# Splitting the mixers' projection weights in the first block only, and loading both parts from device memory afterwards

## The chip, the cores and the metric

The kernel runs on one core of a Trainium2 chip. The metric is the device time of one launch in microseconds (us); the time before is the median of three runs. A core has five engines that each work through an instruction list of their own: PE (TensorE, matrix multiplication), DVE (VectorE), ACT (ScalarE), POOL (GpSimd) and SP (SyncE, which here issues nearly all DMAs). They meet at semaphores. DMAs bring data between device memory and the on-chip memory (SBUF); PE writes its sums into PSUM.

## The reference

One layer of a streaming encoder, for a prompt of 2048 rows and a sample of 32 rows, each row 1024 wide:

```
xn   = rms_norm(x);  proj = xn @ w_in          # 1024 x 2176
u_a, u_b, u_c, u_d = split(proj)               # 512, 896, 256, 512 columns
y_a = conv module(u_a)      # gate, causal depthwise conv of width 31, layer norm, swish
y_b = RWKV-7 mixer(u_b)     # token shift, decay, delta-rule state, 4 heads of 64
y_c = pooling mixer(u_c)    # trailing means of 2/4/8/16 rows
y_d = window attention(u_d)
x   = x + concat(y_a, y_b, y_c, y_d) @ w_out   # 1024 x 1024
x   = x + (silu(rms_norm(x) @ gate) * (rms_norm(x) @ up)) @ down
```

The outputs are both x and the caches and states of both. All values are float32.

## The kernel before

**Three products for one.** A float32 operand is written as a rounded part and a remainder (`hi` and `lo`, type fp32r), and `mm3` (line 92) computes hi·hi + hi·lo + lo·hi. Every weight and every activation that enters such a product has to be split first: ACT copies the raw values to the fp32r type, which rounds them, and another engine subtracts the copy from the raw values.

**Stages.** The mixers come first, then the feed-forward part in two stages (gate and up; down). The mixer stage walks over the prompt in eight blocks of 256 rows (`TB`, line 46); the sample rides along in block 1. In every block the whole of `w_in` and the whole of `w_out` is needed again. They are taken in units: one unit is 1024 rows by 256 columns (128 columns for one of them), read by `load_unit` (line 358) in two halves of 512 rows, that is, of four k-slices of 128 rows. A block has 13 units: four in `proj_b` (line 439; mixer B's columns, the first unit with 128 columns), five in `proj` (line 474: two for attention in `qkv_half`, two for the convolution, one for pooling), four in `out_proj` (line 1056).

**One unit.** `load_unit` loads each half into a tile `wraw` (three buffers). For each pair of k-slices it allocates `whi` and `wlo` (four buffers each, which hold one unit), has ACT copy `wraw` to `whi` (line 370) and POOL subtract (line 373) to get `wlo`. Three of the subtractions of the first two units are given to DVE (`LV0`, line 75). So a half is one DMA, two ACT instructions and two POOL instructions, and a full one is 128 partitions by 4 by 256 values, 512 KB. The tiles are given back when PE has done its last matmul with them. In `transposed` (line 423) PE goes through all eight k-slices for the first 128 columns and then through all eight again for the next 128; in `qkv_half` through all eight for the first 128 rows of the block and again for the next; in `out_proj` (`KO` = 4) both row tiles use the first half before the second half is touched.

**Order.** The letters of `ORD` (line 68) give the order in which a block's parts are written down: `proj` of block b, recurrence of b, norm and `proj_b` of b+1, preparation of the recurrence of b+1, `out_proj` of b−1, then attention preparation, pooling, convolution, output of mixer B, attention of b. Thus two to three blocks are under way at once. A planner that is part of the program's framework then orders every engine's instructions, by priorities and by a timeline of its own. The splits stand under a raised priority (`EVP`). The DMAs of SP are issued in the planner's order, one after the other, and each waits for its target buffer.

**Neighbours on DVE.** The convolution (line 551) is 60 `scalar_tensor_tensor` instructions a block, each reading two tiles in SBUF. The solve of the recurrence's preparation (lines 830, 833, 835) is some 60 small instructions a block, again with two SBUF inputs. Results of the projections are taken from PSUM by ACT and DVE (lines 461 to 466, 509 to 517, 1091).

Of the kernel before, what the change touches and what calls it, by code (L numbers as in the profile page):

```python
# [8 lines left out]
F32 = mybir.dt.float32  # L9
F32R = mybir.dt.float32r  # L10
BF16 = mybir.dt.bfloat16
AF = mybir.ActivationFunctionType
# [5 lines left out]
ADD, SUB, MUL, MAX = ALU.add, ALU.subtract, ALU.mult, ALU.max  # L18
# [14 lines left out]
def layer(tc, ins, outs):  # L33
    nc = tc.nc
    V, S, G, TE = nc.vector, nc.scalar, nc.gpsimd, nc.tensor
# [3 lines left out]
    KT = D // 128  # L39
# [19 lines left out]
    LOV = ()  # L59
    RP = ""  # L60
    YB = 1
    WR = 3
    WH = 4
    YT = "rk"
    KH = 8
    KI = 8
# [9 lines left out]
    HG = 2  # L76
# [15 lines left out]
    def mm3(out, ah, al, bh, bl, first, last, more=False):  # L92

        TE.matmul(out, ah, bh, start=first, stop=False, skip_group_check=more)  # L94
        TE.matmul(out, ah, bl, start=False, stop=False, skip_group_check=more)  # L95
        TE.matmul(out, al, bh, start=False, stop=last, skip_group_check=more)  # L96

    def mm2(out, ahl, bh, bl, first, last):
        TE.matmul(out, ahl, bh, start=first, stop=False)  # L99
        TE.matmul(out, ahl, bl, start=False, stop=last)  # L100

    def add2(acc, ps):

        V.tensor_tensor(acc, acc, ps[0:DS], op=ADD)
        V.tensor_tensor(acc, acc, ps[DS:2 * DS], op=ADD)

    dpool = ctx.enter_context(tc.tile_pool(name="dram", bufs=1, space=DRAM))
# [41 lines left out]
    b3 = p1.enter_context(tc.tile_pool(name="b3", bufs=2, side="left"))  # L149
# [88 lines left out]
    for e in range(2):  # L238
        o = 64 * e
# [35 lines left out]
    for g, w in enumerate(WINS):  # L275
        o = 64 * (g % 2)
# [15 lines left out]
    for sg in (seg_p, seg_s):  # L292
        sg.mask = tri_mask("tri" + sg.name, sg.CPT, sg.L)
        n = sg.NC * (sg.L + 1)
# [35 lines left out]
    for e in range(2):  # L330
        o = 64 * e
# [23 lines left out]

    nun = [0]

    def load_unit(dma, n):
        parts = []
        dv = LV0[nun[0]] if nun[0] < len(LV0) else LOV  # L360
        nun[0] += 1
        for j in range(0, KT, 4):
            raw = b3.tile([128, 4, 256], F32, tag="wraw", name="wraw", bufs=WR)
            dma(raw, j)
            for i in range(0, 4, HG):
                hi = b3.tile([128, HG, 256], F32R, tag="whi", name="whi", bufs=WH)
                lo = b3.tile([128, HG, 256], F32R, tag="wlo", name="wlo", bufs=WH)
                src = raw[:, i:i + HG, :n]
                with tc.high_priority(offset=EVP):
                    S.activation(hi[:, :, :n], src, AF.Copy)  # L370
                    for q in range(0, HG, 2):
                        e = V if (j + i + q) // 2 in dv else G
                        e.tensor_tensor(lo[:, q:q + 2, :n], src[:, q:q + 2], hi[:, q:q + 2, :n].bitcast(F32), op=SUB)  # L373
                parts.append((hi, lo))
        return lambda k, w: (parts[k // HG][0][:, k % HG, w], parts[k // HG][1][:, k % HG, w])

    def load_win(c0, n):
        return load_unit(lambda r, j: nc.sync.dma_start(
            r[:, :, :n], w_in[j * 128:j * 128 + 512, c0:c0 + n].rearrange("(k p) c -> p k c", p=128)), n)

    ysx = c1.tile([128, 8, 2 * DS], F32R, name="ysx")
# [12 lines left out]
    def sgs(b, o):  # L394
        return [sg for sg in (seg_p, seg_s) if at_block(sg, b, o)]
# [27 lines left out]
    def transposed(b, xh, xl, res, c0, nm, evac):  # L423
        W = TB + DS if b == SB else TB
        wt = load_win(c0, nm * 128)
        pss = {}
        for k0 in range(0, KT, KH):
            for m in range(nm):
                if k0 == 0:
                    pss[m] = pmm.tile([128, 512], F32, tag="mm", name="pj")  # L430
                ps = pss[m]
                for k in range(k0, k0 + KH):
                    mm3(ps[:, :W], *wt(k, slice(m * 128, (m + 1) * 128)), xh[:, k, :W], xl[:, k, :W], k == 0, k == KT - 1)
                if k0 + KH == KT:
                    for sg in segs(b):
                        with tc.high_priority(offset=EVP):
                            evac(sg, res[sg.name], m, ps[:, sg.col:sg.col + sg.T])
# [618 lines left out]
    def out_proj(b, ys):  # L1056
        for q in range(D // 256):
            cw = slice(q * 256, q * 256 + 256)

            def dma(raw, j):  # L1060
                if j == 0:
                    nc.sync.dma_start(raw, w_out[0:512, cw].rearrange("(k p) c -> p k c", p=128))
                    return
                nc.sync.dma_start(raw[:, 0:2, :], w_out[512:768, cw].rearrange("(k p) c -> p k c", p=128))
                for kv in range(2):
                    nc.sync.dma_start(raw[64 * kv:64 * kv + 64, 2:4, :],
                                      w_out[768 + 128 * kv:896 + 128 * kv, cw].rearrange("(g d) c -> d g c", d=64))
            wt = load_unit(dma, 256)
            pss = {}
            for k0, sg, i in ((k0, sg, i) for k0 in range(0, KT, KO) for sg in sgs(b, "O") for i in range(sg.NT)):  # L1070
                PT = sg.PT
                if k0 == 0:
                    src = x_s if sg is seg_s else x_p[b * TB + i * 128:b * TB + i * 128 + 128]
                    xr = b3.tile([128, 256], F32, tag="xr", name="xr", bufs=XRB)
                    nc.sync.dma_start(xr[:PT], src[:, cw])
                    pss[sg.name, i] = pmm.tile([128, 512], F32, tag="mm", name="po"), xr
                ps, xr = pss[sg.name, i]
                cs = slice(i * 128, i * 128 + PT)
                for k in range(k0, k0 + KO):
                    if sg is seg_s:  # L1080
                        mm2(ps[:2 * DS, :256], ysx[:, k, :], *wt(k, slice(0, 256)), k == 0, k == 7)
                        continue
                    yh, yl = ys["abcd"[k // 2]]
                    mm3(ps[:PT, :256], yh[:, k % 2, cs], yl[:, k % 2, cs], *wt(k, slice(0, 256)), k == 0, k == 7)
                if k0 + KO == KT:
                    dst = x2d[SEQ:SEQ + DS] if sg is seg_s else x2d[b * TB + i * 128:b * TB + i * 128 + 128]
                    with tc.high_priority(offset=EVP):
                        if sg is seg_s:
                            add2(xr[:PT], ps[:, :256])
                        else:  # L1090
                            V.tensor_tensor(xr[:PT], ps[:PT, :256], xr[:PT], op=ADD)
                    nc.sync.dma_start(dst[:, cw], xr[:PT])
# [8 lines left out]
    for b in range(NB):  # L1101
        ys = y_tiles()
        cur = res
        for o in ORDS[max(b - NB, -len(ORDS))]:
          with tc.high_priority(offset=OFF[o]) if o in OFF else ExitStack():
            if o == "R":
                ro = mix_b(b, cur, ys)
            if o == "Y":
                mix_y(ro, ys)
            if o == "O" and pend is not None:  # L1110
                out_proj(*pend)
            if o == "A":
                proj(b, cur, *xhl)
            if o == "P":
                mix_p(b, cur)
            if o == "D":
                mix_d(b, cur, ys)
            if o == "C":
                mix_a(b, cur, ys)
            if o == "L":  # L1120
                mix_c(b, cur, ys)
            if o == "n" and b + 1 < NB:
                xn = norm_load(b + 1)
            if o == "N" and b + 1 < NB:
                xhl = norm(b + 1, xn)
            if o == "B" and b + 1 < NB:
                res = proj_b(b + 1, *xhl)
            if o == "S" and b + 1 < NB:
                for sg in sgs(b + 1, "R") if SEP else [seg_p]:
                    rwkv_prep(sg, rs(sg, res))  # L1130
        pend = (b, ys)
    out_proj(*pend)
    p1.close()

# [179 lines left out]
    for hf in range(D // 512):  # L1314
        w = slice(hf * 512, hf * 512 + 512)
        with tc.high_priority(offset=FNP):
            dws = [down_w(f, w) for f in range(NF)]
        for t in range(TT // 128 + 1):
            n = min(128, TT - t * 128)
# [4 lines left out]
            lo = ah[:, :, n:2 * n] if n == DS else al[:, :, :n]  # L1324
# [56 lines left out]
```

## Time and profile before

| | |
|---|---|
| median of the runs shown | 2809.56 us (three runs, 2804.55 to 2813.81) |
| the profiled execution's own time | 2805.44 us |
| its span, first to last instruction | 2803.7 us |
| mean granted TensorE clock | 0.946 of full speed |
| HBM read, written | 267.69 MB, 40.96 MB |
| DMA packets | 399678, 311.46 MB, mean 111 GB/s |

Span and own time differ by 1.7 us, which lie around the first and the last instruction. A profile row names the source line, the engine, the operation, the tiles written and read, and shapes; then the busy time in us with the mean of one instruction in ns, or, in the views of one tile or one line, the smallest, median and largest duration in ns with the first and last start in us. `wraw`, `whi`, `wlo` are the tiles of the weights; `pj`, `pjd` and `po` the PSUM tiles of `transposed`, `qkv_half` and `out_proj`; `accp` is the convolution's sum, `dn` and `gu` belong to the feed-forward part. A letter p or s behind a name stands for prompt or sample. Idle time stands behind the engine that sat idle, with what ended it.

### The profile page before, as it was taken

To read this page: it belongs to the slowest core of one execution; us is meant where nothing else is said; L and a number is where in the kernel's file an instruction comes from. 1 tells how busy PE (TensorE), PEld (TensorE's weight loads), DVE (VectorE), ACT (ScalarE), POOL (GpSimd) and SP (SyncE) were. 2 spreads that over 40 slices of the span, in tenths; PEclk is the share of its full clock that TensorE was granted. 3 is DMA by queue.
4 is the path that set the end of the run, shared out by engine and by line. 5 is a ranking of instruction groups with operands and counts; after the bars stand their busy time and mean duration, and the time that the engine had idled before them with its cause. 6 is when DMAs were issued, how large, how long until landed. Compare 5 with 4: busy or idle time off the path is not lost. (4 is left out here: it accounts for less than half of the span.)

```text
span 2803.7 us, 44493 instructions
## 1 busy us (share of the span) xinstructions
PE 2525.5 (90%) x16433; PEld 2276.9 (81%) x16433; DVE 1959.7 (70%) x3629; ACT 1152.6 (41%) x2389; POOL 1427.4 (51%) x1093
## 2 busy tenths in 40 slices
PE   7888797888988898886999989999899969999999
PEld 6777676777877787775899989999899967887887
DVE  7897969898797979975877777777766633224221
ACT  5445354453545445454444444444444432112110
POOL 5545545564555655565677757677677720001000
PEclk9889888899999999997999989999999989999999
DMA  4323322332334332435334323333233366446442
GB/s 149 93 62 98 98 85 86 117 99 86 110 103 120 102 102 92 120 110 158 94 108 131 104 81 107 121 103 100 87 114 106 95 180 187 124 118 180 133 125 54
DMA packets 399678, 311.46 MB, mean 111 GB/s; under 512 B 23282, under 2 KB 372739, under 8 KB 399459
## 3 DMA queue, kind: packets, MB, share of 16 engines
q1 hardware_dynamic: 397848, 307.99, 36.7%
q8 instruction: 129, 2.11, 0.3%
q10 hardware_dynamic: 1611, 0.62, 0.1%
q14 instruction: 90, 0.74, 0.1%
HBM read 267.69 MB, written 40.96 MB: 110 GB/s over the span
## 5 line engine op out<-in xcount | busy, mean ns | idle before, releaser
L1223 POOL TENSOR_TENSOR wl<-wf,wh 128x512 fp32r<-128x512 f32 x462 | 665.1, 1444 | 248.9 <-ACT wh L1222 237.8
L373 POOL TENSOR_TENSOR wlo<-wraw,whi 128x512 fp32r<-128x512 f32 (+1 forms) x413 | 566.7, 1391 | 418.4 <-ACT whi L370 341.7
L94 PE MATMUL gu<-xh,wh 128*128 128x352 f32 (+1 forms) x1848 | 595.1, 323 | 27.8 <-ACT xh L1187 18.3
L96 PE MATMUL gu<-xh,wl 128*128 128x352 f32 (+1 forms) x1848 | 597.8, 324 | 0.0
L95 PE MATMUL gu<-xl,wh 128*128 128x352 f32 (+1 forms) x1848 | 595.3, 322 | 0.7 <-DVE xl L1188 0.7
L1222 ACT ACTIVATE wh<-wf 128x512 fp32r<-128x512 f32 x462 | 290.3, 631 | 466.2 <-PE gu L95 397.8
L94 PEld LDWEIGHTS gu<-xh,wh 128*128 128x128 f32 x1848 | 350.0, 190 | 30.2 <-ACT xh L1187 19.2
L95 PEld LDWEIGHTS gu<-xl,wh 128*128 128x128 f32 x1848 | 350.6, 190 | 1.0 <-DVE xl L1188 0.9
L96 PEld LDWEIGHTS gu<-xh,wl 128*128 128x128 f32 x1848 | 350.1, 189 | 0.2
L370 ACT ACTIVATE whi<-wraw 128x512 fp32r<-128x512 f32 (+1 forms) x416 | 247.7, 611 | 196.4 <-PE po L96 68.7
L551 DVE SCALAR_TENSOR_TENSOR accp<-gbp,d_cws,accp 128x256 f32<-128x256 f32 x480 | 308.3, 674 | 0.6
L94 PE MATMUL dn<-dw,ah 128*128 128x512 f32 x704 | 275.1, 392 | 25.0 <-ACT dw L1310 23.7
L96 PE MATMUL dn<-dw,al 128*128 128x512 f32 x704 | 275.0, 391 | 0.9 <-DVE al L1328 0.9
L95 PE MATMUL dn<-dw,ah 128*128 128x512 f32 x704 | 274.2, 391 | 0.0
L94 PE MATMUL pj<-xh,whi 128*128 128x256 f32 (+1 forms) x832 | 253.5, 308 | 14.2 <-DVE gbp L512 7.0
L96 PE MATMUL pj<-xh,wlo 128*128 128x256 f32 (+1 forms) x832 | 250.8, 310 | 13.5 <-POOL wlo L373 13.3
L95 PE MATMUL pj<-xl,whi 128*128 128x256 f32 (+1 forms) x832 | 249.5, 304 | 0.1
L1340 DVE TENSOR_TENSOR xr<-xr,dn 128x512 f32<-128x512 f32 x32 | 22.0, 687 | 306.2 <-PE dn L96 306.2
L1327 ACT ACTIVATE ah<-af 128x1408 fp32r<-128x1408 f32 (+1 forms) x68 | 86.5, 1321 | 362.1 <-PE dn L95 340.2
L94 PEld LDWEIGHTS pj<-xh,whi 128*128 128x128 f32 x832 | 171.0, 206 | 26.0 <-DVE gbp L512 7.5
L96 PEld LDWEIGHTS pj<-xh,wlo 128*128 128x128 f32 x832 | 167.9, 205 | 26.9 <-POOL wlo L373 18.5
L94 PEld LDWEIGHTS dn<-dw,ah 128*128 128x128 f32 x704 | 132.9, 189 | 54.4 <-ACT dw L1310 25.4
(511 smaller groups left out, 5262.2 us busy)
## 6 DMA issues: line engine op xcount, KB each, us to landing
wraw<-in_w_in_dram SPq DMA_DIRECT2D x128, 512.0 KB, 3.8
af<-act_d SPq DMA_DIRECT2D x32, 1408.0 KB, 7.2
wf<-in_ffn_w_gate_dram SPq DMA_DIRECT2D x132, 256.0 KB, 2.9
wf<-in_ffn_w_up_dram SPq DMA_DIRECT2D x132, 256.0 KB, 3.0
wraw<-in_w_out_dram SPq DMA_DIRECT2D x32, 512.0 KB, 4.0
act_d<-act SPq DMA_DIRECT2D x44, 352.0 KB, 2.5
draw<-in_ffn_w_down_dram SPq DMA_DIRECT2D x44, 256.0 KB, 3.3
xt<-in_x_prompt_dram SPq DMA_DIRECT2D x16, 512.0 KB, 4.2
```

The costliest lines, as they stand in the source:

```text
L94: TE.matmul(out, ah, bh, start=first, stop=False, skip_group_check=more)
L95: TE.matmul(out, ah, bl, start=False, stop=False, skip_group_check=more)
L96: TE.matmul(out, al, bh, start=False, stop=last, skip_group_check=more)
L370: S.activation(hi[:, :, :n], src, AF.Copy)
L373: e.tensor_tensor(lo[:, q:q + 2, :n], src[:, q:q + 2], hi[:, q:q + 2, :n].bitcast(F32), op=SUB)
L551: V.scalar_tensor_tensor(acc[:, c, :], gb[:, c, j:j + T], cws[c][:, j:j + 1], acc[:, c, :], op0=MUL, op1=ADD)
L1222: S.activation(hi, q[nm], AF.Copy)
L1223: G.tensor_tensor(lo, q[nm], hi.bitcast(F32), op=SUB)
L1327: S.activation(ah[:, fs_, :n], af[:, fs_, :n], AF.Copy)
L1340: V.tensor_tensor(xr, xr, ps, op=ADD)
```

## The change

In block 0 each unit is loaded and split as before, but both parts go into one tile `whl` (128 partitions by 2 by 4 by 256), and a DMA then writes this tile to a tensor in device memory, one per unit (`kept`). In blocks 1 to 7 (for `out_proj`: its second to eighth call) `load_unit` does nothing else than load both parts of each half from there. `whl` has three buffers, each for both parts of a half; `wraw` has one buffer instead of three; `whi` and `wlo` are gone. Together the tiles take as much SBUF as before: 28 KB a partition. The matmuls and their operands are the same.

```diff
-    WR = 3
-    WH = 4
+    WR, WHB = 1, 3
...
-    def load_unit(dma, n):
+    kept = {}
+
+    def load_unit(key, dma, n):
         parts = []
+        if key in kept:
+            for j in range(0, KT, 4):
+                hl = b3.tile([128, 2, 4, 256], F32R, tag="whl", name="whl", bufs=WHB)
+                nc.sync.dma_start(hl[:, :, :, :n].bitcast(F32), kept[key][j // 4])
+                parts.append(hl)
+            return lambda k, w: (parts[k // 4][:, 0, k % 4, w], parts[k // 4][:, 1, k % 4, w])
+        kept[key] = dpool.tile([KT // 4, 128, 2, 4, n], F32, name="wk_" + key)
         dv = LV0[nun[0]] if nun[0] < len(LV0) else LOV
         nun[0] += 1
         for j in range(0, KT, 4):
             raw = b3.tile([128, 4, 256], F32, tag="wraw", name="wraw", bufs=WR)
             dma(raw, j)
+            hl = b3.tile([128, 2, 4, 256], F32R, tag="whl", name="whl", bufs=WHB)
             for i in range(0, 4, HG):
-                hi = b3.tile([128, HG, 256], F32R, tag="whi", name="whi", bufs=WH)
-                lo = b3.tile([128, HG, 256], F32R, tag="wlo", name="wlo", bufs=WH)
                 src = raw[:, i:i + HG, :n]
                 with tc.high_priority(offset=EVP):
-                    S.activation(hi[:, :, :n], src, AF.Copy)
-                    for q in range(0, HG, 2):
-                        e = V if (j + i + q) // 2 in dv else G
-                        e.tensor_tensor(lo[:, q:q + 2, :n], src[:, q:q + 2], hi[:, q:q + 2, :n].bitcast(F32), op=SUB)
-                parts.append((hi, lo))
-        return lambda k, w: (parts[k // HG][0][:, k % HG, w], parts[k // HG][1][:, k % HG, w])
+                    S.activation(hl[:, 0, i:i + HG, :n], src, AF.Copy)
+                    e = V if (j + i) // 2 in dv else G
+                    e.tensor_tensor(hl[:, 1, i:i + HG, :n], src, hl[:, 0, i:i + HG, :n].bitcast(F32), op=SUB)
+            nc.sync.dma_start(kept[key][j // 4], hl[:, :, :, :n].bitcast(F32))
+            parts.append(hl)
+        return lambda k, w: (parts[k // 4][:, 0, k % 4, w], parts[k // 4][:, 1, k % 4, w])
...
-        return load_unit(lambda r, j: nc.sync.dma_start(
+        return load_unit(f"i{c0}", lambda r, j: nc.sync.dma_start(
...
-            wt = load_unit(dma, 256)
+            wt = load_unit(f"o{q}", dma, 256)
```

## The prediction

> **What bounds the kernel now.** I read the page first (busy times, groups, DMA issues), then the busy time of the engines in stretches, then single lines. The change touches the mixer stage alone, so its end comes first: the last write of `out_proj`.
>
> ```profile
> span 2803.7 us, 44493 instructions
> ...
> L373 POOL TENSOR_TENSOR wlo<-wraw,whi 128x512 fp32r<-128x512 f32 (+1 forms) x413 | 566.7, 1391 | 418.4 <-ACT whi L370 341.7
> ...
> L370 ACT ACTIVATE whi<-wraw 128x512 fp32r<-128x512 f32 (+1 forms) x416 | 247.7, 611 | 196.4 <-PE po L96 68.7
> L551 DVE SCALAR_TENSOR_TENSOR accp<-gbp,d_cws,accp 128x256 f32<-128x256 f32 x480 | 308.3, 674 | 0.6
> ```
>
> ```profile
> L1092 SPq DMA_DIRECT2D x2d<-xr x68: 313/327/585, 308.8 to 1301.2; - x68
> ```
>
> The stage ends at 1302 us; the 1502 us behind it use none of the changed code and stay. Now the stage in 50 us stretches and as a whole (columns: PE, PE's weight loads, DVE, ACT, POOL, granted clock, DMA share, GB/s):
>
> ```profile
> 300.00:350.00 50.00, 35.27 (x310) 32.55 (x309) 49.79 (x111) 16.56 (x38) 28.84 (x23) 0.91 0.35 106
> ...
> 850.00:900.00 50.00, 46.72 (x340) 41.45 (x338) 35.72 (x84) 26.68 (x63) 29.77 (x26) 0.97 0.36 106
> 950.00:1000.00 50.00, 42.65 (x329) 37.75 (x329) 49.79 (x106) 17.42 (x39) 31.21 (x25) 0.90 0.37 116
> 1000.00:1050.00 50.00, 45.30 (x317) 40.15 (x316) 33.95 (x85) 25.16 (x60) 26.51 (x23) 0.90 0.33 96
> ```
>
> ```profile
> 920.00:1075.00 155.00, 139.60 (x1067) 119.86 (x1066) 134.24 (x300) 77.16 (x187) 96.04 (x74) 0.93 0.34 103
> ...
> 1230.00:1302.00 72.00, 64.14 (x464) 51.58 (x463) 34.21 (x73) 37.67 (x94) 47.95 (x42) 0.98 0.48 150
> sum 1302.00, PE 1111.31 PEld 964.42 DVE 1107.88 ACT 625.61 POOL 727.16; mean PE 123.48 PEld 107.16 DVE 123.10 ACT 69.51 POOL 80.80
> ```
>
> Two engines share the bound. About a third of a block's time DVE is full (49.8 of 50 us) and PE is not; in the rest PE stands at 45 to 47 and DVE at 34 to 36. POOL and ACT, from which the change takes work, are full nowhere. So POOL's 566.7 us are not the gain. What counts is what they do to DVE:
>
> ```profile
> L551 DVE SCALAR_TENSOR_TENSOR accp<-gbp,d_cws,accp x480: 431/474/1584, 118.6 to 1228.8; 128x256 f32<-128x256 f32 x160
> ```
>
> ```profile
> L512 DVE SCALAR_TENSOR_TENSOR gbp<-gbp,pj x16: 409/416/423, 95.6 to 1176.3; 128x256 f32<-128x256 f32 x16
> ```
>
> Same operation, same shape. Line 512 reads one input from PSUM and always takes 0.42 us; line 551 reads both from SBUF, takes 0.47 us in the median, up to 1.58 us, and 0.674 us in the mean. The excess of the longest, 1.1 us, is about one POOL subtraction. The second row shows the block's period too: line 512's sixteen instructions run from 95.6 to 1176.3 us, seven periods of some 154 us.
>
> The Trainium skill has a rule for this ("SBUF — State Buffer", section "🔬 SBUF: two separate sides"): DVE and GpSimd share one pair of SBUF ports as an exclusive lock, held for a whole instruction, and a DVE instruction with two SBUF inputs is among those that wait for it. The two rows agree, to the point that the PSUM reader shows no spread.
>
> **The change, part by part.** Blocks are 8, units 13 a block, so the first-time units are 1/8 of all; 7/8 of the splits go.
>
> *DVE's waits.* Mean less median, times count, for the largest groups with two SBUF inputs:
>
> ```profile
> L835 DVE TENSOR_TENSOR t4p<-t4p,t2p 128x60 f32<-128x60 f32 (+19 forms) x184 | 70.4, 383 | 4.3
> L833 DVE TENSOR_TENSOR t2p<-t4p,eep 128x60 f32<-128x60 f32 (+19 forms) x184 | 68.8, 374 | 4.4
> L830 DVE SCALAR_TENSOR_TENSOR t4p<-eep,t4p 128x31 f32<-128x31 f32 (+5 forms) x96 | 37.6, 431 | 0.6
> ```
>
> ```profile
> L835 DVE TENSOR_TENSOR t4p<-t4p,t2p x184: 166/222/1368, 74.1 to 1173.3; 128x60 f32<-128x60 f32 x24, 128x66 f32<-128x66 f32 x16, 128x69 f32<-128x69 f32 x8, 128x63 f32<-128x63 f32 x8
> ```
>
> ```profile
> L833 DVE TENSOR_TENSOR t2p<-t4p,eep x184: 173/223/1344, 72.8 to 1173.1; 128x60 f32<-128x60 f32 x24, 128x66 f32<-128x66 f32 x16, 128x69 f32<-128x69 f32 x8, 128x63 f32<-128x63 f32 x8
> ```
>
> ```profile
> L830 DVE SCALAR_TENSOR_TENSOR t4p<-eep,t4p x96: 212/237/1370, 69.4 to 1147.5; 128x27 f32<-128x27 f32 x16, 128x26 f32<-128x26 f32 x16, 128x25 f32<-128x25 f32 x16, 128x24 f32<-128x24 f32 x16
> ```
>
> That is 480 x 0.200 = 96, 184 x 0.161 = 30, 184 x 0.151 = 28 and 96 x 0.194 = 19 us: 173 us in four rows. The same subtraction over all DVE groups of these 1302 us, some 300 with their shapes, comes to about 270 us, of DVE's 1108. Not all of it is line 373's: that line is 567 of POOL's 727 busy us, 78%. So 210 to 270 us, and 7/8 of them, 184 to 236 us, go: 26 to 34 us a block. I take 30.
>
> *What of that reaches the end.* In the stretches where DVE is full, all of it; 60 convolution instructions at 0.2 us make 12 us a block there. In the others PE is the fuller engine, and DVE's results only release it sooner; of the other 18 us I take 60%, 11. The bounds are none and all. Sum: **23 us a block, 161 us over seven blocks**. PE then becomes the next bound. It has room: its back-to-back matmuls start 0.12 us apart, so a unit's 48 matmuls need 5.8 us of the 154/13 = 12 us that a unit now has.
>
> ```profile
> 612.17 0.28 PE L95 MATMUL pj<-xl,whi 128*128 128x256 f32 x1
> 612.29 0.28 PE L96 MATMUL pj<-xh,wlo 128*128 128x256 f32 x1
> 612.41 0.28 PE L94 MATMUL pj<-xh,whi 128*128 128x256 f32 x1
> ```
>
> *ACT and POOL.* ACT loses 364 of 416 copies (7/8 of 247.7 = 217 us), POOL 7/8 of its subtractions. Both have idle time (626 and 727 busy of 1302), so I count nothing for them beyond DVE's waits, except at the stage's end: in the last 72 us DVE does 34 and POOL 48, and `out_proj` of the last block waits there for splits. I take 4 us, bounds 0 and 15.
>
> *The loads that replace the splits.* A half is now 1 MB in one load instead of 512 KB.
>
> ```profile
> wraw<-in_w_in_dram SPq DMA_DIRECT2D x128, 512.0 KB, 3.8
> af<-act_d SPq DMA_DIRECT2D x32, 1408.0 KB, 7.2
> ```
>
> ```profile
> L378 SPq DMA_DIRECT2D wraw<-in_w_in_dram x144: 367/368/758, 2.2 to 1181.4; - x144
> ```
>
> No row has a 1 MB load. Between 3.8 us for 512 KB and 7.2 us for 1408 KB lies 5.7 us on a line; with the issue of 0.37 us, 6.1 us (the line's ends, 4.2 and 7.6, are the bounds). Capacity holds: a block moves 155 x 103 GB/s = 16 MB now and 12.5 MB more afterwards, 28.5 MB in some 132 us or 216 GB/s, which at 0.34 busy for 103 GB/s is a share of 0.71. What may not hold is the lead. Before, a unit's splits needed some 2 us (0.61 + 1.39) once PE had given a tile back. Now the three `whl` tiles hold one and a half units, and the second half of the next unit can only be asked for when PE has left the first half of this one. In `transposed` and `qkv_half`, nine units a block, that is at three quarters of the unit, and PE needs it at one quarter of the next: half a unit's time. At 12 us a unit this is 6.0 us, at 10.2 us (132/13) 5.1 us, so up to 1 us is short, 9 us a block. Where DVE is full this wait costs nothing, and the planner has other PE work between the units. I take 2 us a block, **14 us**; the bounds are 0 and the slow case below. In `out_proj` the first half is left at mid-unit and the lead is a whole unit: nothing. What stands behind a waiting load on SP is the next load, `xt`, `xr` and the writes of `x2d`, each due a good part of a block later.
>
> *Block 0.* With one `wraw`, DMA and split no longer overlap: 3.8 + 0.4 + 0.6 + 2 x 1.4 = 7.6 us a half. The nine units up to the pooling columns are 18 halves, so the last is split at about 2 + 18 x 7.6 = 139 us; now its results leave PSUM at 105.6 us:
>
> ```profile
> L515 ACT ACTIVATE ucp<-pj x16: 362/368/387, 105.6 to 1211.6; 128x256 f32<-128x256 f32 x16
> ```
>
> So 30 us late, of which a part is hidden, since DVE starts the convolution only at 118.6 us now. I take **25 us** (bounds 0 and 45; the eight halves of the first `out_proj` need 61 us of the next block, which has them). The 26 writes of 1 MB are in this phase too; they release `whl` late, but three tiles at 7.6 us are 23 us for a write of some 6. Nothing for them, up to 10.
>
> *Sum.* 161 + 4 − 14 − 25 = 126 us. From the profiled execution's own 2805.4 us: 2679. The median of the runs shown lies 4 us above that execution; **2683 us**.
>
> **The rivals.**
>
> *Full relief.* All 34 us a block come through, PE keeping up, block 0 costs 10: 238 + 4 − 10 = 232, so 2577. For it: PE needs only 13 x 5.8 = 75 us a block for projections. Against: PE is busy 140 of 155 us.
>
> *PE holds.* PE's busy time, 140 of 155, does not shrink, because it is the chain of its own small products; with some load waits the block takes 142, a gain of 13: 91 + 4 − 14 − 25 = 56, so 2753. For it: the stretches with PE at 45 to 47 of 50. Against: these busy times contain the time in which a lone matmul drains (0.28 us for one, 0.12 in a row), which shrinks when work comes denser.
>
> *Nothing moves.* DVE's relief only becomes DVE's idle time outside the full stretches, and block 0 and the loads eat the rest (5 x 7 − 25 − 10 = 0): 2809.
>
> *Slower: the short ring.* Place: the nine units a block in which PE sweeps both halves twice. If the planner lays them back to back (5.8 us each), the lead is 2.9 us, and with a load of 7.6 us PE waits 4.7 us a unit. With two thirds of the 63 units so, 197 us in place of the 14: 126 + 14 − 197 = −57, so 2866. It decides from 140 us on, 2.2 us a unit. Against: units stand 12 us apart, with mixer work between.
>
> The Trainium skill adds to this case ("TensorE: Matmul & The Clock Gate", section "Part 1: The HAM clock gate (the "warmup" mystery)"): about 3.4 us without work halve PE's clock until it has been busy as long again. The granted clock of 0.90 where DVE is full against 0.97 at 850 to 900 us fits that; by it waits of 4.7 us would cost still more, and the forecast case a little less than summed here.
>
> **How the numbers follow.** Forecast 0.55, full relief 0.17, PE holds 0.16, nothing moves 0.04, slower 0.08. Range: from the full relief's time to above PE's, 2575 to 2780, which leaves out the last two cases and the lower part of the second, somewhat under 0.2. A measurement of this kernel can tell about 0.3% (8 us) from no change. Faster by more: 0.55 + 0.17 + 0.16 = 0.88; within: 0.04; slower: 0.08.
>
> **What would show it.** Line 373 at 52 instructions or fewer, line 551's mean near 0.47 us in blocks 1 to 7, DVE's busy time in the stage down by some 180 to 240 us; line 551 of block 0 still with its waits. Block period near 132 us (line 512's first and last start). PE's waits for DMAs of `whl` under 30 us in total; the loads landing in 4 to 6 us. The results of block 0's pooling unit at some 135 us. Wrong would be: line 551 still at 0.6 us (the lock was another's), PE waiting on `whl` by 140 us or more (short ring), or PE's busy time per block at 132 us and more with DVE below 110 (PE holds).

## The result, and the profile after

| | before | after |
|---|---|---|
| median | 2810.81 us (4 runs) | 2703.61 us (4 runs, 2697.44 to 2708.03) |
| span of the profiled execution | 2803.7 us | 2702.9 us |

The ratio is 0.9625, with a 95% interval of 0.961 to 0.964: about 107 us faster. The forecast was 2683 us in a range of 2575 to 2780.

Line numbers move in the changed kernel (loads from device memory 364, writes to it 380, raw loads 385, the first block's split 377 and 379, gate results 519, convolution 558). From its page come the busy times, the traffic and the convolution's group. POOL's instructions were 1093 before.

```profile
span 2702.9 us, 43107 instructions
...
PE 2478.9 (92%) x16433; PEld 2252.7 (83%) x16433; DVE 1689.2 (62%) x3629; ACT 966.0 (36%) x2025; POOL 922.2 (34%) x729
...
HBM read 359.44 MB, written 67.18 MB: 158 GB/s over the span
...
L558 DVE SCALAR_TENSOR_TENSOR accp<-gbp,d_cws,accp 128x256 f32<-128x256 f32 x480 | 223.7, 502 | 0.5
```

The convolution's instruction now takes 0.502 us in the mean, against 0.674. PE's instructions are the same 16433. The kernel now reads 92 MB more from HBM, which is the loads of both parts, and writes 26 MB more, which is block 0's split tiles.

The mixer stage, by its busy times in stretches of the changed kernel (PE, PE's weight loads, DVE, ACT, POOL, clock, DMA share, GB/s):

```profile
0.00:200.00 200.00, 128.00 (x800) 111.26 (x800) 85.03 (x304) 58.88 (x139) 60.17 (x67) 0.78 0.53 168
200.00:350.00 150.00, 140.73 (x1168) 124.67 (x1168) 126.65 (x402) 63.45 (x184) 26.60 (x27) 0.97 0.53 189
...
950.00:1100.00 150.00, 146.80 (x1251) 132.29 (x1249) 116.83 (x360) 56.81 (x151) 19.37 (x21) 0.99 0.64 229
1100.00:1200.00 100.00, 86.77 (x669) 73.42 (x667) 47.07 (x139) 32.16 (x92) 18.07 (x19) 0.94 0.66 228
sum 1200.00, PE 1061.06 PEld 935.92 DVE 837.97 ACT 438.43 POOL 228.63; mean PE 132.63 PEld 116.99 DVE 104.75 ACT 54.80 POOL 28.58
```

The sum gives DVE 838 busy us in the stage, 270 less than the 1108 before. In the later blocks PE is the full engine (146.8 of 150 us from 950 us on), at a granted clock of 0.99. The first row is the other half of the story: in the first 200 us no engine is full. PE has 128 of 200 us, DVE 85.

Where the 103 us of the stage come from is told by two lines, the gate results of the convolution's unit (two instructions a block, eight blocks) and the last write of the stage:

```profile
L519 DVE SCALAR_TENSOR_TENSOR gbp<-gbp,pj x16: 412/419/423, 169.7 to 1073.8; 128x256 f32<-128x256 f32 x16
```

```profile
L1099 SPq DMA_DIRECT2D x2d<-xr x68: 317/326/1217, 345.4 to 1198.1; - x68
```

| | first gate result | seven periods | from the last one to the stage's last write |
|---|---|---|---|
| before | 95.6 | 1080.7 (154.4 each) | 124.9 |
| after | 169.7 | 904.1 (129.2 each) | 124.3 |
| difference | +74.1 | −176.6 | −0.6 |

The seven periods run from the line's first start to its last. So the blocks give 177 us (25 each), and the beginning takes 74 of them back. These two starts are the measure for all experiments below.

### The profile page after: what moved, and what is told of

Read it like the earlier page. It is cut to its first block, busy times and chain, and to the rows that moved or that the text cites. A ratio compares the mean times of both kernels' runs of the same rounds, so it can differ in the third digit from the quotient of the medians.

```text
span 2702.9 us, 43107 instructions
## 1 busy us (share of the span) xinstructions
PE 2478.9 (92%) x16433; PEld 2252.7 (83%) x16433; DVE 1689.2 (62%) x3629; ACT 966.0 (36%) x2025; POOL 922.2 (34%) x729
## 5 line engine op out<-in xcount | busy, mean ns | idle before, releaser
L93 PE MATMUL pj<-xh,whl 128*128 128x256 f32 (+1 forms) x832 | 256.1, 309 | 33.7 <-ACT whl L377 22.5
L95 PE MATMUL pj<-xh,whl 128*128 128x256 f32 (+1 forms) x832 | 248.3, 302 | 2.9 <-POOL whl L379 2.7
L94 PE MATMUL pj<-xl,whl 128*128 128x256 f32 (+1 forms) x832 | 250.9, 302 | 0.1
L558 DVE SCALAR_TENSOR_TENSOR accp<-gbp,d_cws,accp 128x256 f32<-128x256 f32 x480 | 223.7, 502 | 0.5
L93 PEld LDWEIGHTS pj<-xh,whl 128*128 128x128 f32 x832 | 169.4, 204 | 48.6 <-ACT whl L377 25.2
L93 PEld LDWEIGHTS dn<-dw,ah 128*128 128x128 f32 x704 | 133.6, 190 | 56.1 <-ACT dw L1317 24.7
L95 PEld LDWEIGHTS pj<-xh,whl 128*128 128x128 f32 x832 | 167.3, 203 | 8.3 <-POOL whl L379 4.3
L94 PEld LDWEIGHTS pj<-xl,whl 128*128 128x128 f32 x832 | 169.6, 204 | 5.2 <-issue 3.1
L95 PEld LDWEIGHTS dn<-dw,al 128*128 128x128 f32 x704 | 133.4, 189 | 29.0 <-DVE al L1335 1.4
```

The costliest lines, as they stand in the source:

```text
L558: V.scalar_tensor_tensor(acc[:, c, :], gb[:, c, j:j + T], cws[c][:, j:j + 1], acc[:, c, :], op0=MUL, op1=ADD)
```

## The experiments

All times are medians of four executions (six for the ring of two). Each was timed beside the kernel before, which stood at 2805.9 us beside four of them (the write, the subtraction, the copy, the ring of quarters) and at 2807.5 us beside the others. Beside the changed kernel it stood at 2810.8 us, so a difference from the changed kernel's 2703.61 us can be off by some 5 us.

### The write behind the next load

```diff
+    late = []
...
             dma(raw, j)
+            while late:
+                late.pop()()
...
-            nc.sync.dma_start(kept[key][j // 4], hl[:, :, :, :n].bitcast(F32))
+            late.append(lambda d=kept[key][j // 4], t=hl: nc.sync.dma_start(d, t[:, :, :, :n].bitcast(F32)))
```

> One edit: in the first block the write of a split half is issued behind the load of the next raw half, not ahead of it. Theory A, the write and the next raw load share a DMA queue and the load waits for the 1 MB in front of it: the time of one half in block 0 falls from about 10 us to 7.5 to 8 us, the pooling results of block 0 leave PSUM some 35 to 45 us earlier than in the changed kernel, and the time falls from 2704 to about 2665 us. Theory B, only the single raw buffer matters (load, then split, then load) and the write costs nothing: a half stays at 10 us and the time stays within 6 us of 2704.

Measured: 2654.62 us, ratio to before 0.9459 (0.9445 to 0.9473), 49 us less than the changed kernel. The raw loads of block 0 are 18 in both kernels; first and last start of their line, in the changed kernel and in this one:

```profile
L385 SPq DMA_DIRECT2D wraw<-in_w_in_dram x18: 385/427/1807, 2.3 to 176.9; - x18
```

```profile
L390 SPq DMA_DIRECT2D wraw<-in_w_in_dram x18: 367/368/434, 2.3 to 136.9; - x18
```

That is 17 steps of 10.3 us against 17 of 7.9. One step shows where the difference lies. The changed kernel's SP and ACT (start, duration):

```profile
90.63 0.33 SPq L380 DMA_DIRECT2D wk_i<-whl  x1
91.00 1.81 SPq L385 DMA_DIRECT2D wraw<-in_w_in_dram  x1
```

```profile
97.67 1.15 ACT L377 ACTIVATE whl<-wraw 128x512 fp32r<-128x512 f32 x2 [8.59 <-DMA wraw<-in_w_in_dram]
```

and the experiment's:

```profile
87.99 0.37 SPq L390 DMA_DIRECT2D wraw<-in_w_in_dram  x1
88.40 0.50 SPq L385 DMA_DIRECT2D wk_i<-whl  x1
```

```profile
92.58 1.15 ACT L382 ACTIVATE whl<-wraw 128x512 fp32r<-128x512 f32 x2 [6.41 <-DMA wraw<-in_w_in_dram]
```

From the start of the load's issue to the first copy of it 6.7 us pass where 1 MB was issued just ahead of it, and 4.6 us where it goes behind; in both, ACT waited for this load alone. The first of these issues is a slow one (1.81 us). Over all sixteen full halves of block 0's first nine units the medians are 6.1 and 4.5 us.

```profile
L524 DVE SCALAR_TENSOR_TENSOR gbp<-gbp,pj x16: 400/422/423, 133.6 to 1022.6; 128x256 f32<-128x256 f32 x16
```

The first gate result comes at 133.6 us in place of 169.7. The periods sum to 889.0 us, 15 less than in the changed kernel. So the order of the two issues is worth 36 us at the beginning and 15 later, which fits theory A; B falls. What the load does behind the write, wait in one queue or share the engines with it, is not shown.

### The subtraction stays

The raw values are written beside the rounded ones, and POOL subtracts in every block.

```diff
                 nc.sync.dma_start(hl[:, :, :, :n].bitcast(F32), kept[key][j // 4])
+                for i in range(0, 4, HG):
+                    with tc.high_priority(offset=EVP):
+                        x = hl[:, 1, i:i + HG, :n]
+                        G.tensor_tensor(x, x.bitcast(F32), hl[:, 0, i:i + HG, :n].bitcast(F32), op=SUB)
...
-            nc.sync.dma_start(kept[key][j // 4], hl[:, :, :, :n].bitcast(F32))
+            nc.sync.dma_start(kept[key][j // 4][:, 0], hl[:, 0, :, :n].bitcast(F32))
+            nc.sync.dma_start(kept[key][j // 4][:, 1], raw[:, :, :n])
```

> The raw values are kept beside the rounded ones, and POOL subtracts in every block, in place, as it did before the change; the copies by ACT stay away, the loads stay as large. Theory, the gain is DVE no longer waiting behind POOL's subtractions: the convolution's instruction goes back from a mean of 0.50 to about 0.65 us, DVE's busy time in the mixer stage rises by some 200 us, and the time rises by 150 to 190 us, to 2855 to 2895 us, above the kernel before. Rival, the gain is ACT's and POOL's own queues being shorter or the projections starting earlier: under 60 us more than the changed kernel.

Measured: 2850.80 us, ratio to before 1.0156 (1.0139 to 1.0173), 147 us above the changed kernel, just under the range. Its convolution and its gate line:

```profile
L563 DVE SCALAR_TENSOR_TENSOR accp<-gbp,d_cws,accp 128x256 f32<-128x256 f32 x480 | 302.3, 659 | 0.4
```

```profile
L524 DVE SCALAR_TENSOR_TENSOR gbp<-gbp,pj x16: 389/415/421, 131.5 to 1214.2; 128x256 f32<-128x256 f32 x16
```

The seven periods are back at 1082.7 us, 154.7 each; before it was 154.4. All that the blocks had gained is gone, though ACT's copies are still away. The stretch behind the last gate result is 11 us longer too. (Block 0 is 38 us earlier here than in the changed kernel, probably since its raw values are written in a DMA of 512 KB of their own, at another place; with block 0 as late as there the time would lie in the range.)

### The copy stays

The same the other way: raw values beside the remainders, ACT rounds in every block.

```diff
+                        x = hl[:, 0, i:i + HG, :n]
+                        S.activation(x, x.bitcast(F32), AF.Copy)
...
+            nc.sync.dma_start(kept[key][j // 4][:, 0], raw[:, :, :n])
+            nc.sync.dma_start(kept[key][j // 4][:, 1], hl[:, 1, :, :n].bitcast(F32))
```

> The raw values are kept beside the remainders, and ACT rounds them in every block, in place; POOL's subtractions stay away, the loads stay as large. Theory, ACT's copies cost nothing because ACT has room: the convolution's mean stays at 0.50 us and the time rises by 0 to 25 us (PE waits 0.6 us more for a tile). Rival, the shorter ACT queue carries much of the gain: 50 us or more above the changed kernel.

Measured: 2682.83 us, ratio 0.9559 (0.9545 to 0.9573): 21 us *below* the changed kernel, outside both expectations. The gate line tells where:

```profile
L524 DVE SCALAR_TENSOR_TENSOR gbp<-gbp,pj x16: 402/421/423, 149.3 to 1053.0; 128x256 f32<-128x256 f32 x16
```

The seven periods are 903.7 us, as in the changed kernel (904.1): ACT's 364 copies cost the blocks nothing. The 20 us are at the beginning, 149.3 against 169.7, where only 512 KB are issued directly ahead of the next raw load. It is, in effect, the first experiment at half the dose; no run separates this from the other write's new place.

### A subtraction that nobody waits for

In the second experiment PE also got its tiles later. Here POOL subtracts into a buffer that nobody reads.

```diff
+                no = b3.tile([128, 4, 256], F32, tag="wraw", name="wno", bufs=WR)
+                for i in range(0, 4, HG):
+                    with tc.high_priority(offset=EVP):
+                        G.tensor_tensor(no[:, i:i + HG, :n], hl[:, 1, i:i + HG, :n].bitcast(F32), hl[:, 0, i:i + HG, :n].bitcast(F32), op=SUB)
```

> On top of the changed kernel, POOL does the subtractions in blocks 1 to 7 from the loaded tile into a buffer that nobody reads (364 extra instructions, no result changes; PE does not wait for them). This separates the second experiment's two possible costs. Theory, DVE's waiting behind POOL is the cost: the convolution's mean returns to 0.63 to 0.67 us and the time rises by 110 to 160 us over the changed kernel's 2704, to 2815 to 2865 us. Rival, the second experiment was slow because PE had to wait for tiles that were split late: under 50 us, 2755 us or less.

Measured: 2885.31 us, ratio 1.028 (1.0258 to 1.0302), 182 us above the changed kernel and 20 above the range. Its gate line:

```profile
L523 DVE SCALAR_TENSOR_TENSOR gbp<-gbp,pj x16: 406/416/422, 168.8 to 1239.3; 128x256 f32<-128x256 f32 x16
```

The periods sum to 1070.5 us (152.9 each), nearly those of before; another 14 us come behind the last gate result. The rival falls: PE's waiting for late tiles isn't needed for the loss. POOL also holds each loaded tile longer here, but PE's waits for the loads are 10 us between 300 and 1370 us, not more than the changed kernel's 16 (below).

### A fill in place of the subtraction

```diff
+                        G.tensor_copy(no[:, i, 0:1], hl[:, 1, i, 0:1].bitcast(F32))
+                        for _ in range(2):
+                            G.memset(no[:, i:i + HG, :n], 0.0)
```

> As the run before, but POOL fills the unread buffer with zeros, twice for each pair of slices, behind a copy of one column that waits for the load: POOL is kept about as busy or busier, and reads next to nothing from SBUF. If DVE waits only behind POOL instructions that read SBUF, the convolution's mean stays at 0.50 to 0.53 us and the time within 30 us of 2704. If it waits behind any POOL instruction, the mean rises as in the run before, in proportion to POOL's busy time, and the time by 80 us or more.

Measured: 2697.09 us, ratio 0.9615 (0.9598 to 0.9633), the changed kernel's within the spread of both. POOL's and DVE's rows over the stage, of this run:

```profile
L370 POOL MEMSET wno<- 128x512 f32 (+1 forms) x728 | 342.3, 511 | 0.0
L368 POOL COPY wno<-whl 128x1 f32<-128x1 f32 x364 | 101.0, 309 | 263.3 <-DMA whl<-wk_i 173.6 <-DMA whl<-wk_o 86.9
```

```profile
L564 DVE SCALAR_TENSOR_TENSOR accp<-gbp,d_cws,accp 128x256 f32<-128x256 f32 x480 | 221.9, 497 | 0.6
```

and of the run before, to set beside it:

```profile
L368 POOL TENSOR_TENSOR wno<-whl 128x512 f32<-128x512 f32 (+1 forms) x364 | 476.7, 1329 | 301.9 <-DMA whl<-wk_i 172.9 <-DMA whl<-wk_o 126.1
```

```profile
L562 DVE SCALAR_TENSOR_TENSOR accp<-gbp,d_cws,accp 128x256 f32<-128x256 f32 x480 | 295.8, 648 | 0.6
```

443 us of POOL work that hardly reads SBUF leave the convolution at 0.497 us; 477 us that read two tiles bring it to 0.648. The single fills are shorter than the subtractions, so a wait behind them would be shorter too; but there is none to see, with 0.497 us here and 0.502 in the changed kernel. A longer list of work for POOL costs nothing here either. So a busy POOL is not what DVE waits for. The Trainium skill says so ("SBUF — State Buffer", section "Who interferes with whom"): a DVE instruction with two SBUF inputs contends with a GpSimd instruction that reads SBUF, not with one that only writes it. The two runs agree.

### The ring of two

```diff
-    WR, WHB = 1, 3
+    WR, WHB = 1, 2
```

> The changed kernel with two tiles for loaded halves instead of three, so that in the sweeps of both halves a load can start only when PE leaves a half. Theory, a load takes about 5 us from issue to landing: nine units a block wait about 5 us less what the planner hides, so 25 to 45 us a block and 180 to 320 us in all over 2704. Rival, the lead does not matter because other PE work always stands between the units: under 60 us more.

Measured: 2782.38 us, ratio 0.9912 (0.9879 to 0.9945), 79 us above the changed kernel: between the two expectations. The profiled execution is the fastest of the six, at 2767.12 us. Its gate line:

```profile
L519 DVE SCALAR_TENSOR_TENSOR gbp<-gbp,pj x16: 411/422/424, 168.2 to 1141.3; 128x256 f32<-128x256 f32 x16
```

The periods sum to 973.1 us, 139.0 each, 10 us more a block. The ring's length has a price, but less than half of the least that was expected. That other work of PE stands between the units would explain it; no run shows this. Of the changed kernel's own ring of three, this is what PE waits for it from 300 to 1190 us (total, times, longest):

```profile
PE pjd L93 <- DMA whl<-wk_i: 7.3, 5, 3.3
PE po L93 <- DMA whl<-wk_o: 7.3, 6, 2.9
...
PE pj L93 <- DMA whl<-wk_i: 1.2, 2, 1.0
```

That is 16 us. With the ring of two, the same three waits are 61 us from 300 to 1255 us, 36 of them in `po`.

### The ring of quarters

The same 28 KB as seven tiles of a quarter unit. A raw half of block 0 lies in one of the seven, and the writes go behind the next load.

```diff
-    WR, WHB = 1, 3
+    WHB = 7
...
+            for j in range(0, KT, 2):
+                nc.sync.dma_start(part()[:, :, :, :n].bitcast(F32), kept[key][j // 2])
...
+            raw = b3.tile([128, 4, 256], F32, tag="whl", name="wraw", bufs=WHB)
```

Here `part()` allocates one tile of 128 by 2 by 2 by 256 from the ring; the first block's splits fill such tiles, two for each raw half.

> The same 28 KB as seven tiles of a quarter unit (512 KB each, both parts), which also hold the raw halves of block 0; writes behind the next raw load as in the first experiment. Theory A with the short ring of little weight: block 0 gains what the first experiment gains or 10 us more, because the next raw half can be loaded while one is split, and blocks 1 to 7 gain at most the 15 us that PE waits for these loads: 2640 to 2665 us. Rival, the ring of three halves holds PE up in blocks 1 to 7 beyond the waits that are seen: 2600 us or less.

Measured: 2624.85 us, ratio 0.9354 (0.934 to 0.9368), 79 us below the changed kernel and 30 below the first experiment: between the two expectations.

```profile
L527 DVE SCALAR_TENSOR_TENSOR gbp<-gbp,pj x16: 409/422/425, 105.5 to 980.0; 128x256 f32<-128x256 f32 x16
```

The first gate result is at 105.5 us, 28 us before the first experiment's and 10 us behind the kernel before. The periods are 874.5 us, 124.9 each, 4 us a block less than in the changed kernel. So nearly all of the lost beginning comes back, more than the 10 us that were expected beyond the first experiment. The blocks gain 30 us, but three things differ from the changed kernel: the smaller tiles, the raw halves in the ring, and the order of the writes. The first experiment, with the order alone, already has 15 of the 30. The other 14 are near what PE is seen to wait: its waits for the loads fall from 19.5 us in the first experiment (264 to 1140 us) to 8.3 (237 to 1108 us). So waits beyond those that are seen, the rival, found no support. In this run the stretch behind the last gate result is 9 us longer than in the changed kernel.

Then every second subtraction of block 0 was given to DVE as well (`LOV = (1, 3)`):

> The ring of quarters (2625 us) with every second subtraction of block 0 given to DVE, which has idle time there. If POOL's subtractions still set the pace of block 0, its pooling results leave PSUM 10 us or more earlier than at 130 us and the time falls by 8 to 20 us, to 2605 to 2617. If the loads set it, within 5 us of 2625.

Measured: 2613.35 us, ratio 0.9302 (0.9275 to 0.9329), the fastest of all. Whether by the reason given is not settled. Its profiled execution, the slowest of its four, has a span of 2620.0 us, the other's, the fastest of its four, 2619.8. In it the first gate result is 8.5 us earlier (97.0 us) and the first pooling result 8.7 us (110.3 against 119.0), less than the 10 that were expected, and the periods are 3 us longer each. The 130 us in the expectation are where the convolution starts in the ring of quarters, not its pooling results.

## Why the prediction was right, and where it was off

**DVE's waits (26 to 34 us a block, 23 of them reaching the end): right.** The periods shrank by 25 us. The subtraction alone brings all of it back (154.7 us a period with it, ACT's copies still away), and nearly all even where its result is thrown away (152.9). DVE's busy time fell by 270 us, more than the 184 to 236 forecast. The four rows that the prediction lists fell by 85, 26, 25 and 14 us, 150 together, where 7/8 of 173 is 151; so mean less median was right for them, and the surplus lies in the many smaller groups. Why those gave more is not shown.

**What limits next (PE): right.** The period was forecast at 132 us and is 129, with PE at 146.8 of 150. PE's busy time did shrink, to 1061 us from 1111; that is why the case "PE holds" failed. Its granted clock rose too, from 0.92 in the mean of 350 to 1230 us to 0.96 over 350 to 1100. How much of the 50 us is the clock and how much denser work is not separated. The prediction tied a clock of 0.90 to a full DVE; its own row from 1000 to 1050 us has 0.90 with DVE at 34 of 50, so that tie is loose. Of DVE's 270 us only 177 became time: by then PE stood at 146.8 of 150.

**ACT and POOL for themselves (0, and 4 us at the end): right, and the end within its bounds.** Copies kept in all blocks leave the period at 129.1. The end of the stage gained 0.6 us.

**The loads (14 us): right in size, not in place.** PE's seen waits are 16 us between 300 and 1190 us. But 7 of them are in `out_proj` (`po`), for which the prediction said "nothing", and only 1 in `transposed` (`pj`). The case "short ring" did not come: it needed 197 us. The ring of two shows that a shorter lead does cost time, at 10 us a block, with 36 of PE's 61 us of waits in `out_proj`.

**Block 0 (25 us, bounds 0 and 45): wrong, 74 us.** The failing step is the sentence on the writes, "Nothing for them, up to 10." The split itself was sized well: 7.6 us a half were forecast, and without a write ahead of the load it is 7.9. With the write there it is 10.3. The pooling unit's results, forecast at some 135 us, came at 189.1. The writes were weighed only by how long they hold `whl`; that SP issues them directly ahead of the next raw load, which with one raw buffer is the one transfer that everything waits for, was not looked at. Over the 17 steps that is 40 us. When the order was turned, the first gate result came 36 us earlier and the whole time fell by 49. The rest of the 74, 38 us, goes with the single raw buffer's own serial chain: the ring of quarters, which takes this chain apart, leaves 10. The prediction also counted on part of the lateness being hidden by DVE's other work; DVE was busy 85 us of the first 200, so there was little to hide it behind.

In the stage the sum of 126 us stands against 103 measured. Behind it stand two larger errors: the blocks gave 177 us in place of 147 with the loads, and the beginning cost 74 in place of 25. That they partly cancel is luck; the forecast is 20 us off where its terms are off by 30 and 49.

## What to carry to other kernels

Before pricing an engine's removed work by its busy time, look for who waits behind it: here some 500 us of POOL work, on an engine that was never full, cost some 25 us a block through another engine's instructions, and the spread between the median and the largest duration of one line, beside a line of the same shape that reads PSUM, showed it in advance. When a cache is filled in the first pass, price that pass by its own chain: which buffer it has one of, and what is issued directly ahead of the transfer that fills it. Cut a ring's memory into smaller pieces before asking for more of it: the same 28 KB in quarters, holding the raw halves too, gave 28 us in block 0 and 14 in the other blocks on top of the write's new place.

## What the runs showed of the hardware

That a load of 512 KB issued by SP right behind a write of 1 MB was usable 1.6 us later (in the median 6.1 against 4.5 us) was not expected. POOL's fills of 128 by 512 values (some of 128 by 256) took 0.51 us in the mean and cost DVE nothing, where its subtractions of the same sizes took 1.33 us and cost the convolution's instruction 0.15 us in the mean.
